# Attention: the low-part score pass on all 128 rows, weighted values 256 columns wide

## The chip, the cores and the metric

The kernel runs on one core of one Trainium2 chip. The metric is the device time of one execution in microseconds, as the median of three runs; the profile is one further execution, whose span runs from its first to its last instruction.

## The reference

Two layers over 256 latent tokens and 256 context tokens of width 1024. Each layer has three branches on one shared projection: an mLSTM, a windowed attention with a sink logit, and a global attention with normalised queries and keys; both attentions have 8 query heads on 2 key heads, head width 64. A gated sum of the branches and a SwiGLU block follow. What the change touches is the middle of both attentions:

```python
scale = d ** -0.5
s = jnp.einsum('bgrqd,bgkd->bgrqk', qblk, k_all).astype(jnp.float32) * scale
p = jax.nn.softmax(s, axis=-1).astype(v_all.dtype)
return jnp.einsum('bgrqk,bgkd->bgrqd', p, v_all)
```

In layer 0 latent queries read all 512 tokens and context queries the 256 context tokens; in layer 1 there are latent queries alone.

## The kernel before

All data is float32. Projections are made of three products of a high and a low part (type F32R, `mm3`): high x high, high x low, low x high. Scores are split in the same way, but a head has 64 features only, so `finish_qk` packs parts by partition. For queries the tile of head group g has the high part on partitions 64 g to 64 g + 63 and the low part on the other half. For keys the tile `k[g]` has the high part of group g on both halves, and one third tile `k2` has the low part of group 0 on partitions 0 to 63 and of group 1 on 64 to 127. `scores` then makes two passes for each group into one PSUM bank: 128 rows (query high and low by key high), and 64 rows (query high by key low).

`attention` walks over units: pair of heads (4), latent or context queries, query block `qb` of 128 queries (2). That is 16 units for each attention in layer 0 and 8 in layer 1, 48 in all. Each unit has two groups g. At each step PE gets the scores of the next unit, the transposes of the last unit's probabilities (`transposed`, into the two PSUM buffers `tr`), some filler (gate projections and merges of other branches, the list `fill`), and the weighted values (`values`). ScalarE copies each transposed tile into a `pt` buffer. `values` multiplies, for each block of 128 keys and each group, a value tile of 64 columns by the transposed probabilities of 128 queries; group 0 goes to PSUM partitions 0 to 63 and group 1 to 64 to 127 of `acc`. These operands are plain float32. After both query blocks `acc` is split into a high and a low part for the merge.

The order on each engine is set once, when the kernel is built: a scheduler takes instructions by priority, and the scores are raised (`urgent`), so they are put between other work, also between the passes of the filler, of the transposes and of the values. On the chip each engine then works through its own list and waits on semaphores. Weight blocks come in by DMA, are split by ScalarE (L192, `whi`) and VectorE (L193, `wlo`), and run ahead of their use. Modulation loads for later use share the pool `q` with queries and keys.

Of the kernel before, what the change touches and what calls it, by code (L numbers as in the profile page):

```python
# [38 lines left out]
# feature blocks of the input projection, in the order in which they are packed  # L39
# [5 lines left out]
# the gates have a bias row only: their weights come apart  # L45
# [3 lines left out]
# columns of the packed shape constants  # L49
# [4 lines left out]
# columns of the packed small parameters  # L54
# [25 lines left out]
class Blank:  # L80
    """Stands for the chip while the order of the weight blocks is collected."""
# [11 lines left out]
class Net:  # L93
    def __init__(self, nc, tc, es, io, out, plan=None):
        self.nc, self.tc, self.io, self.out = nc, tc, io, out
        self.n = 0
        self.plan, self.used, self.sent, self.ready, self.ahead = plan, [], 0, {}, 0
        pool = lambda name, bufs, **kw: es.enter_context(tc.tile_pool(name=name, bufs=bufs, **kw))
        self.cp = pool("cp", 1)
        self.pools = {  # L100
            "wraw": pool("wraw", 5), "wlo": pool("wlo", 8), "whi": pool("whi", 8),
            "hx": pool("hx", 16), "m": pool("m", 9), "y": pool("y", 16), "wk": pool("wk", 5), "pt": pool("pt", 4),
            "q": pool("q", 12), "n": pool("n", 3), "g": pool("g", 2), "h": pool("h", 6),
            "sm": pool("sm", 12), "sn": pool("sn", 6), "sc": pool("sc", 8),
        }
        for name, bufs in (("mm", 3), ("s", 2), ("tr", 2), ("acc", 1)):
            self.pools[name] = pool(name, bufs, space=PSUM)
        self.cst = self.cp.tile([128, NCST], F32, name="cst")
        self.sp = self.cp.tile([128, NSP], F32, name="sp")
        self.X = self.cp.tile([128, NKB, T], F32, name="X")  # L110
        self.hb = self.cp.tile([128, 2, NW_IN - B_O], F32, name="hb")
        self.b1 = self.cp.tile([128, 8], F32, name="b1")
        self.gk = self.cp.tile([128, 52], F32, name="gk")
        self.gqb = self.cp.tile([128, 8], F32, name="gqb")
        self.hmg = self.cp.tile([128, 8], F32, name="hmg")
        self.nsk = self.cp.tile([128, 16], F32, name="nsk")
        self.sel = self.cp.tile([128, 64], F32R, name="sel")
        self.sel2 = self.cp.tile([128, 8], F32R, name="sel2")
        self.dup = self.cp.tile([128, 48], F32, name="dup")
        self.low = self.cp.tile([128, 1], F32, name="low")  # L120
        self.ident = self.cst[:, C_ID:C_ID + 128]
        self.ones = self.cst[:, C_ONE:C_ONE + 1]
        self.bd = self.cst[:, C_BD:C_BD + 2]
        self.cos = self.cst[:, C_COS:C_COS + 256]
        self.sin = self.cst[:, C_SIN:C_SIN + 256]
# [21 lines left out]
    def weights(self, name, idx, kb=8, width=128):  # L147
        """High and low parts of a block in pieces of width columns, fetched in the order in which they are used."""
# [46 lines left out]
    def rms_columns(self, parts, n, inv, cols, nc_):  # L195
        """1 / sqrt(mean + EPS) of every token, up to the factor RS_K that the gains carry, tokens on the partitions.

        parts: squares, features on the partitions; cols: [128, nc_] picks the features of each group."""
# [22 lines left out]
    def inv_rms(self, parts, n, inv, cols, nc_, tag):  # L221
        """The same on all the partitions, tokens along the free axis."""
# [66 lines left out]
    def mod_dve(self, blk):  # L289
        """One block of the modulation: features on the partitions, sums along the free axis."""  # L290
# [109 lines left out]
    def proj_v(self, l, hx):  # L400
        """Values of all the heads of the mLSTM, tokens on the partitions."""
# [15 lines left out]
    def proj_values(self, l, hx):  # L417
        """Values of both attentions, tokens on the partitions: by two blocks of tokens, then by attention."""
# [46 lines left out]
    def finish_qk(self, f, sq, n, gain, keys):  # L465
# [21 lines left out]
        k2 = self.big("q", F32R)  # L487
        c = k2[:, :n]
        for g, x in enumerate((a, b)):
            own = slice(64 * g, 64 * g + 64)  # L490
            for to in (0, 64):
                nc.scalar.activation(out=x[to:to + 64], in_=f[own], func=AF.Copy)
            nc.vector.tensor_tensor(out=c[own], in0=f[own], in1=x[own].bitcast(F32), op=ALU.subtract)
        return hi, lo, k2

# [6 lines left out]
    def gate_part(self, ps, w, k, x):  # L502
        """One feature block of the 16 gate columns; four blocks side by side on the array."""
        r = 32 * (k % 4)
        self.mm(ps[r:r + 32], w[:, 32 * k:32 * k + 32], x, k < 4, k >= 4)
# [54 lines left out]
    def stack_rows(self, rows, n):  # L560
        """Rows as F32R high parts on partitions 0-63 and low parts on 64-127."""
# [10 lines left out]
    def mlstm_weights(self, h, n, rows):  # L572
        """Decay weights by (direction, source block): the tile and the columns that hold them."""
# [53 lines left out]
    def mlstm_heads(self, n, q, k, v, rows, den, other):  # L627
        """Numerators of all the heads; the scores run one half of the source blocks ahead of the values."""
# [33 lines left out]
    def mlstm_sum(self, h, n, nums, r, sums):  # L662
        """Both directions of a head together, and the sums of its squares as rows: high and low parts of a
        row lie 16 partitions apart."""
# [39 lines left out]
    def scores(self, l, pair, q, k, ctx, window, qb):  # L704
        nc = self.nc
# [4 lines left out]
        for g in range(2):  # L710
            ks = slice(64 * g, 64 * g + 64)
# [3 lines left out]
            self.mm(s[:, :nk], q[g][ks, qs], k[2][ks, k0:T], False, True)  # L715
# [25 lines left out]
    def transposed(self, ps, ctx):  # L741
        nk = SEQ if ctx else T
        nb = nk // 128
        pts = []
        for p in ps:
# [3 lines left out]
            pts.append(self.big("pt"))  # L749
            self.nc.scalar.activation(out=pts[-1][:, :nk], in_=pt[:, :nk], func=AF.Copy)  # L750
        return pts

    def values(self, pts, v, window, ctx, qb, acc):
        k0 = SEQ if ctx else 0
        nb = (T - k0) // 128
        for b in range(nb):
            vb = k0 // 128 + b
            c = 256 * (vb % 2) + (0 if window else 128)
            for g in range(2):
                self.mm(acc[64 * g:64 * g + 64, 128 * qb:128 * qb + 128],  # L760
                        v[vb // 2][:, c + 64 * g:c + 64 * g + 64],
                        pts[g][:, 128 * b:128 * b + 128], b == 0, b == nb - 1)

    def attention(self, l, heads, n, ys, fill):
        """heads: (pair, q, k, v, window) by name of the result; one unit of scores runs ahead of the values."""
# [3 lines left out]
        acc = None  # L769
        prev = None  # L770
        done = 0
        for u in range(len(units) + 1):
# [6 lines left out]
            if prev is not None:  # L779
                pts = self.transposed(prev[0], prev[2])  # L780
# [3 lines left out]
            if prev is not None:  # L784
                _, v, ctx, qb, i = prev
                if qb == 0:
                    acc = self.big("acc")
                self.values(pts, *v, ctx, qb, acc)
                if qb == 1:
# [74 lines left out]
    def scaled_hx(self, hx, l, j):  # L864
        """The block before the norm's factor, and the shift as the columns after it."""
# [381 lines left out]
def build(arrays):  # L1247
    nc = bacc.Bacc("TRN2", target_bir_lowering=False, num_devices=1)
# [15 lines left out]
```

## Time and profile before

| | |
|---|---|
| runs | 1526.5, 1526.93, 1527.32 us; median 1526.93 |
| profiled execution | span 1523.1 us, first to last instruction; the median of the runs is 3.8 us more |
| PE (matmul) | busy 1507.0 us, 8999 records |
| VectorE, ScalarE | busy 1067.4 and 748.9 us |
| attention, layer 0 | scores and values from 219 to 492 us |
| attention, layer 1 | from 1106 to 1263 us |

Matmuls overlap in the records: each record lasts from its start to the end of its pipeline, so busy time and mean duration don't say how long PE is kept. The distance between two starts does. In a timeline row "x3" stands for three records of one kind in a row, beginning at the start that is given. A shape "64\*128" in such a row is the rows by columns of the array that are used, and what follows is the output.

### The profile page before, as it was taken

What the parts mean: (1) busy time and instruction counts of PE and PEld (TensorE: products, weight loads), DVE (VectorE), ACT (ScalarE), POOL (GpSimd) and SP (SyncE); (2) the same over time, 40 slices, a digit from 0 to 9 for tenths busy, and PEclk for the clock granted to TensorE, in tenths of its full rate; (3) what the DMA queues carried; (4) which work ended last, traced back from release to release, by engine and by line L of the source; (5) the groups of instructions that cost most, each with busy time, mean ns of one, the idle gap of its engine ahead of it and who ended that gap; (6) DMA issues with size and microseconds to landing.
All of it is one profiled execution on the core that took longest, in us unless ns stands there. A gap on an engine that the chain in (4) does not pass through costs nothing.

```text
span 1523.1 us, 25242 instructions
## 1 busy us (share of the span) xinstructions
PE 1507.0 (99%) x8999; PEld 1241.7 (82%) x9000; DVE 1067.4 (70%) x2664; ACT 748.9 (49%) x1525; POOL 31.1 (2%) x72
## 2 busy tenths in 40 slices
PE   8999999999999999999999999999999999999997
PEld 4586677777777889888888888887788889999997
DVE  5396397666558846889588677654788766776765
ACT  4444455555574334532233233653556665665553
POOL 0001100000000000000000000000100000000000
PEclk9999999999999999999999999999999999999999
DMA  9472012112125632466455553341133335566662
GB/s 333 164 237 76 24 50 91 56 62 63 63 83 180 187 97 78 151 215 209 151 193 185 189 173 118 95 131 57 59 112 111 98 105 160 168 192 182 182 179 91
DMA packets 112591, 203.74 MB, mean 134 GB/s; under 512 B 12496, under 2 KB 16336, under 8 KB 112464
## 3 DMA queue, kind: packets, MB, share of 16 engines
q1 hardware_dynamic: 112464, 202.11, 42.0%
q8 instruction: 71, 1.16, 0.3%
q14 instruction: 56, 0.46, 0.1%
HBM read 201.02 MB, written 1.05 MB: 133 GB/s over the span
## 4 chain that ended last, share of the span: by engine, by line
PE 98%; DVE 1%; ACT 0%; issue 0%; DMA 0%; ACTq 0%; DVEq 0%
PE mm L135 65%; PE s L135 21%; PE acc L135 5%; PE tr L135 4%; PE tr L748 3%; DMA h<-w_if 0%; DVE h L1059 0%; ACT m L372 0%; DVE wlo L193 0%; ACT hx L192 0%; ACT whi L192 0%; DVE y L669 0%; DVE q L485 0%; ACT h L274 0%; PE tr L555 0%
## 5 line engine op out<-in xcount | busy, mean ns | idle before, releaser
L192 ACT ACTIVATE whi<-wraw 128x512 fp32r<-128x512 f32 (+1 forms) x558 | 345.7, 625 | 515.3 <-PE mm L135 352.9
L135 PE MATMUL mm<-hx,whi 128*128 128x512 f32 (+2 forms) x2128 | 548.6, 344 | 1.9 <-ACT hx L192 1.6
L193 DVE TENSOR_TENSOR wlo<-wraw,whi 128x512 fp32r<-128x512 f32 (+1 forms) x558 | 374.4, 681 | 171.8 <-ACT whi L192 159.8
L135 PEld LDWEIGHTS mm<-hx,whi 128*128 128x128 f32 x2128 | 364.6, 189 | 60.8 <-issue 15.0
L135 PE MATMUL mm<-hx,wlo 128*128 128x512 f32 (+2 forms) x1064 | 362.3, 341 | 0.1
L135 PE MATMUL mm<-y,whi 128*128 128x256 f32 (+1 forms) x1024 | 259.7, 332 | 0.0
L135 PEld LDWEIGHTS mm<-hx,wlo 128*128 128x128 f32 x1064 | 201.1, 189 | 26.5 <-issue 4.4
L135 PE MATMUL s<-hx,whi 128*128 128x512 f32 (+2 forms) x800 | 193.5, 331 | 0.0
L135 PEld LDWEIGHTS mm<-y,whi 128*128 128x128 f32 x1024 | 176.6, 190 | 18.5 <-issue 1.5
L135 PE MATMUL mm<-y,wlo 128*128 128x256 f32 (+1 forms) x576 | 188.6, 328 | 0.0
L135 PEld LDWEIGHTS s<-hx,whi 128*128 128x128 f32 x800 | 135.6, 189 | 16.2 <-issue 2.9
L135 PE MATMUL s<-hx,wlo 128*128 128x512 f32 (+2 forms) x400 | 132.6, 332 | 0.5 <-DVE wlo L193 0.5
L135 PEld LDWEIGHTS mm<-y,wlo 128*128 128x128 f32 x576 | 109.5, 190 | 10.0 <-issue 0.5
L298 DVE SCALAR_TENSOR_TENSOR q<-q,q 128x512 f32<-128x512 f32 x160 | 105.4, 689 | 0.1
L298 DVE SCALAR_TENSOR_TENSOR h<-q,q 128x512 bf16<-128x512 f32 x160 | 104.7, 688 | 0.1
L135 PE MATMUL mm<-m,whi 128*128 128x256 f32 (+1 forms) x320 | 85.2, 320 | 0.0
L135 PEld LDWEIGHTS s<-hx,wlo 128*128 128x128 f32 x400 | 75.6, 189 | 10.2 <-issue 2.5
L135 PE MATMUL s<-q,q 128*128 128x512 f32 (+1 forms) x192 | 80.0, 424 | 0.0
L750 ACT ACTIVATE pt<-tr 128x512 f32<-128x512 f32 (+1 forms) x96 | 46.7, 525 | 29.6 <-PE tr L748 29.0
L135 PEld LDWEIGHTS mm<-m,whi 128*128 128x128 f32 x320 | 56.9, 190 | 4.4
L823 DVE SCALAR_TENSOR_TENSOR X<-mm,m,X 128x256 f32<-128x256 f32 x88 | 40.2, 482 | 24.8 <-PE mm L135 24.6
L135 PEld LDWEIGHTS s<-q,q 128*128 128x128 f32 x192 | 36.1, 188 | 24.8 <-issue 21.0
(233 smaller groups left out, 1771.8 us busy)
## 6 DMA issues: line engine op xcount, KB each, us to landing
wraw<-w_ff SPq DMA_DIRECT2D x256, 256.0 KB, 3.0
wraw<-w_in SPq DMA_DIRECT2D x206, 256.0 KB, 2.7
q<-w_mod SPq DMA_DIRECT2D x160, 256.0 KB, 3.0
wraw<-w_br SPq DMA_DIRECT2D x48, 256.0 KB, 2.7
y<-w_mod SPq DMA_DIRECT2D x32, 256.0 KB, 5.4
wraw<-w_o SPq DMA_DIRECT2D x32, 256.0 KB, 2.7
X<-x SPq DMA_DIRECT2D x4, 512.0 KB, 5.3
q<-cc SPq DMA_DIRECT2D x8, 256.0 KB, 4.7
```

The costliest lines, as they stand in the source:

```text
L135: self.nc.tensor.matmul(out, a, b, start=start, stop=stop)
L192: nc.scalar.activation(out=hi, in_=x, func=AF.Copy)
L193: return nc.vector.tensor_tensor(out=lo, in0=x, in1=hi.bitcast(F32), op=ALU.subtract)
L298: nc.vector.scalar_tensor_tensor(out=junk if v == 0 else raw, in0=raw, scalar=1.0, in1=self.cb[v][c], op0=ALU.mult, op1=ALU.mult, accum_ou ...
L748: self.nc.tensor.transpose(pt[:, 128 * b:128 * b + 128], p[:, 128 * b:128 * b + 128], self.ident)
L750: self.nc.scalar.activation(out=pts[-1][:, :nk], in_=pt[:, :nk], func=AF.Copy)
L823: nc.vector.scalar_tensor_tensor(out=self.X[:, j, a:b], in0=ps[:, a - c0:b - c0], scalar=self.mod[l][which][:, j, v:v + 1], in1=self.X[:, ...
```

## The change

`finish_qk` makes two low-part tiles for the keys, one for each group, with the same low part on both halves; `scores` uses all 128 rows in the second pass, so the product of the two low parts is added as well. `attention` keeps the transposed probabilities of both query blocks in one pair of tiles (pool `pv`, two buffers of 1024 columns, blocks of keys by 256 queries), and calls `values` once for both blocks, 256 columns wide. The pool `q` has 15 buffers instead of 12, and a scratch size of the builder is smaller. Comments are dropped.

```diff
-            "q": pool("q", 12), "n": pool("n", 3), "g": pool("g", 2), "h": pool("h", 6),
+            "q": pool("q", 15), "pv": pool("pv", 2), "n": pool("n", 3), "g": pool("g", 2), "h": pool("h", 6),
...
-        k2 = self.big("q", F32R)
-        c = k2[:, :n]
+        lows = [self.big("q", F32R) for _ in range(2)]
         for g, x in enumerate((a, b)):
             own = slice(64 * g, 64 * g + 64)
             for to in (0, 64):
                 nc.scalar.activation(out=x[to:to + 64], in_=f[own], func=AF.Copy)
-            nc.vector.tensor_tensor(out=c[own], in0=f[own], in1=x[own].bitcast(F32), op=ALU.subtract)
-        return hi, lo, k2
+            for to in (0, 64):
+                nc.vector.tensor_tensor(out=lows[g][to:to + 64, :n], in0=f[own], in1=x[own].bitcast(F32),
+                                        op=ALU.subtract)
+        return hi, lo, *lows
...
             self.mm(s[:, :nk], q[g][:, qs], k[g][:, k0:T], True, False)
-            self.mm(s[:, :nk], q[g][ks, qs], k[2][ks, k0:T], False, True)
+            self.mm(s[:, :nk], q[g][:, qs], k[2 + g][:, k0:T], False, True)
...
-    def transposed(self, ps, ctx):
-        nk = SEQ if ctx else T
-        nb = nk // 128
-        pts = []
-        for p in ps:
+    def transposed(self, ps, ctx, qb, pts):
+
+        nb = (SEQ if ctx else T) // 128
+        for p, to in zip(ps, pts):
             pt = self.big("tr")
             for b in range(nb):
                 self.nc.tensor.transpose(pt[:, 128 * b:128 * b + 128], p[:, 128 * b:128 * b + 128], self.ident)
-            pts.append(self.big("pt"))
-            self.nc.scalar.activation(out=pts[-1][:, :nk], in_=pt[:, :nk], func=AF.Copy)
-        return pts
+            self.nc.scalar.activation(
+                out=to.rearrange("p (b q) -> p b q", q=SEQ)[:, :nb, 128 * qb:128 * qb + 128],
+                in_=pt[:, :128 * nb].rearrange("p (b q) -> p b q", q=128), func=AF.Copy)
...
             for g in range(2):
-                self.mm(acc[64 * g:64 * g + 64, 128 * qb:128 * qb + 128],
-                        v[vb // 2][:, c + 64 * g:c + 64 * g + 64],
-                        pts[g][:, 128 * b:128 * b + 128], b == 0, b == nb - 1)
+                self.mm(acc[64 * g:64 * g + 64, :SEQ], v[vb // 2][:, c + 64 * g:c + 64 * g + 64],
+                        pts[g][:, SEQ * b:SEQ * b + SEQ], b == 0, b == nb - 1)
...
             if prev is not None:
-                pts = self.transposed(prev[0], prev[2])
+                if prev[3] == 0:
+                    pts = [self.t("pv", [128, 4 * SEQ]) for _ in range(2)]
+                self.transposed(prev[0], prev[2], prev[3], pts)
...
-                if qb == 0:
+                if qb == 1:
                     acc = self.big("acc")
-                self.values(pts, *v, ctx, qb, acc)
-                if qb == 1:
+                    self.values(pts, *v, ctx, acc)
```

The scores of one unit on PE, in the global attention of layer 0, before. `s` is the score bank, the two `q` behind the arrow are keys and queries, `mm` is a gate projection that serves as filler.

```order
L135 MATMUL s_4225<-q_2257,q_3186 128x512
L135 MATMUL mm_4137<-hx_258,whi_3977 128x512
L135 MATMUL s_4225<-q_2290,q_3186 128x512
L135 MATMUL mm_4137<-hx_259,whi_3977 128x512
L135 MATMUL mm_4137<-hx_258,wlo_3978 128x512
L135 MATMUL mm_4137<-hx_260,whi_3983 128x512
L135 MATMUL mm_4137<-hx_261,whi_3983 128x512
L135 MATMUL mm_4137<-hx_260,wlo_3984 128x512
L135 MATMUL s_4235<-q_2258,q_3187 128x512
L135 MATMUL mm_4137<-hx_262,whi_3983 128x512
L135 MATMUL s_4235<-q_2290,q_3187 128x512
```

The same place after the change:

```order
L135 MATMUL s_4139<-q_2263,q_3152 128x512
L135 MATMUL mm_4055<-hx_257,wlo_3906 128x512
L135 MATMUL s_4139<-q_2296,q_3152 128x512
L135 MATMUL mm_4055<-hx_259,whi_3905 128x512
L135 MATMUL mm_4055<-hx_260,whi_3905 128x512
L135 MATMUL mm_4055<-hx_259,wlo_3906 128x512
L135 MATMUL mm_4055<-hx_261,whi_3905 128x512
L135 MATMUL mm_4055<-hx_262,whi_3905 128x512
L135 MATMUL s_4149<-q_2264,q_3153 128x512
L135 MATMUL mm_4055<-hx_261,wlo_3906 128x512
L135 MATMUL s_4149<-q_2297,q_3153 128x512
```

The order is the same; the second pass of the two groups reads one shared tile before (`q_2290`, half of it each) and two tiles after (`q_2296`, `q_2297`).

The weighted values on PE, a little further on in the same stage, before; `acc` is the output, `pt` the transposed probabilities, `tr` the transposes of the next unit:

```order
L135 MATMUL mm_4137<-hx_266,wlo_3984 128x512
L135 MATMUL acc_4081<-pt_4115,q_2040 64x128
L135 MATMUL acc_4081<-pt_4122,q_2040 64x128
L135 MATMUL acc_4081<-pt_4115,q_2040 64x128
L135 MATMUL acc_4081<-pt_4122,q_2040 64x128
L135 MATMUL acc_4081<-pt_4115,q_2042 64x128
L135 MATMUL acc_4081<-pt_4122,q_2042 64x128
L135 MATMUL acc_4081<-pt_4115,q_2042 64x128
L135 MATMUL acc_4081<-pt_4122,q_2042 64x128
L748 MATMUL tr_4195<-cst,wk_4093 128x128 x2
```

After the change, the values of the same pair of heads and both query blocks:

```order
L135 MATMUL mm_4055<-hx_269,wlo_3912 128x512
L135 MATMUL acc_4081<-pv_3969,q_2046 64x256
L135 MATMUL acc_4081<-pv_3970,q_2046 64x256
L135 MATMUL acc_4081<-pv_3969,q_2046 64x256
L135 MATMUL acc_4081<-pv_3970,q_2046 64x256
L135 MATMUL acc_4081<-pv_3969,q_2048 64x256
L135 MATMUL acc_4081<-pv_3970,q_2048 64x256
L135 MATMUL acc_4081<-pv_3969,q_2048 64x256
L135 MATMUL acc_4081<-pv_3970,q_2048 64x256
L749 MATMUL tr_4116<-cst,wk_4013 128x128 x2
```

Before, such a run stands once for each unit; after, once for two units, with outputs twice as wide, and the next transposes stand behind it in both.

The key preparation on VectorE in layer 0, before and after (`q` is the low part of the keys, `h` another chain):

```order
L193 TENSOR_TENSOR wlo_1928<-wraw_1926,whi_1927 128x512
L493 TENSOR_TENSOR q_1885<-n_1876,q_1878 64x512
L211 TENSOR_SCALAR h_1903<-h_1902 128x256
L193 TENSOR_TENSOR wlo_1982<-wraw_1980,whi_1981 128x512
L493 TENSOR_TENSOR q_1885<-n_1876,q_1879 64x512
L213 TENSOR_TENSOR h_1904<-h_1902,h_1903 128x256
```

```order
L193 TENSOR_TENSOR wlo_1934<-wraw_1932,whi_1933 128x512
L493 TENSOR_TENSOR q_1888<-n_1879,q_1881 64x512 x2
L211 TENSOR_SCALAR h_1909<-h_1908 128x256
L493 TENSOR_TENSOR q_1889<-n_1879,q_1882 64x512 x2
L213 TENSOR_TENSOR h_1910<-h_1908,h_1909 128x256
L193 TENSOR_TENSOR wlo_1988<-wraw_1986,whi_1987 128x512
```

Each copy stands twice, and one weight split has moved behind them.

## Rows read from the trace of the kernel before

**Rows 1.** The page: engine busy time, share and instructions; chain that ended last.

```profile
PE 1507.0 (99%) x8999; PEld 1241.7 (82%) x9000; DVE 1067.4 (70%) x2664; ACT 748.9 (49%) x1525; POOL 31.1 (2%) x72
...
PE 98%; DVE 1%; ACT 0%; issue 0%; DMA 0%; ACTq 0%; DVEq 0%
```

**Rows 2.** Windows: stretch, length, busy us of PE, PEld, DVE, ACT, POOL, clock, DMA share.

```profile
219.00:492.00 273.00, 273.00 (x1502) 202.15 (x1501) 182.26 (x548) 156.58 (x354) 4.16 (x5) 1.00 0.26 83
1100.00:1130.00 30.00, 29.99 (x199) 25.60 (x199) 25.64 (x73) 16.94 (x38) 0.00 (x0) 1.00 0.36 111
```

**Rows 3.** Waits of PE, whole run, longest: total us, times, longest us.

```profile
PE acc L135 <- DVE sn L218: 1.6, 1, 1.6
```

**Rows 4.** Groups of L135 on PE by form: min/median/max ns, first and last start.

```profile
L135 PE MATMUL acc<-pt,q x640: 272/273/324, 250.5 to 1261.9; 128*64 128x128 f32 x160
...
L135 PE MATMUL s<-q,q x192: 276/396/503, 219.6 to 1248.0; 128*128 128x512 f32 x64, 64*128 64x512 f32 x64, 128*128 128x256 f32 x32, 64*128 64x256 f32 x32
```

**Rows 5.** PE's timeline, layer 0, scores among projections: start, length, engine, instruction, count.

```profile
306.46 0.39 PE L135 MATMUL s<-q,q 128*128 128x512 f32 x1
306.69 0.39 PE L135 MATMUL mm<-hx,whi 128*128 128x512 f32 x1
307.00 0.49 PE L135 MATMUL s<-q,q 64*128 64x512 f32 x1
307.43 0.50 PE L135 MATMUL mm<-hx,whi 128*128 128x512 f32 x1
307.77 0.40 PE L135 MATMUL mm<-hx,wlo 128*128 128x512 f32 x1
```

**Rows 6.** PE's timeline, layer 0, scores among transposes.

```profile
251.05 0.33 PE L748 MATMUL tr<-cst,wk 128*128 128x128 f32 x1
251.13 0.36 PE L135 MATMUL s<-q,q 128*128 128x256 f32 x1
251.33 0.27 PE L748 MATMUL tr<-cst,wk 128*128 128x128 f32 x1
251.53 0.38 PE L135 MATMUL s<-q,q 64*128 64x256 f32 x1
251.84 0.88 PE L748 MATMUL tr<-cst,wk 128*128 128x128 f32 x6
```

**Rows 7.** PE's timeline, layer 0, a value run of 8 passes and the projection behind.

```profile
253.08 0.66 PE L135 MATMUL acc<-pt,q 128*64 128x128 f32 x8
253.67 0.73 PE L135 MATMUL mm<-hx,whi 128*128 128x512 f32 x2
254.24 0.39 PE L135 MATMUL mm<-hx,wlo 128*128 128x512 f32 x1
```

**Rows 8.** PE's timeline, layer 0, a value run of 16 passes.

```profile
285.95 0.39 PE L135 MATMUL mm<-hx,wlo 128*128 128x512 f32 x1
286.26 1.09 PE L135 MATMUL acc<-pt,q 128*64 128x128 f32 x16
287.29 0.33 PE L748 MATMUL tr<-cst,wk 128*128 128x128 f32 x1
```

**Rows 9.** PE's timeline, mLSTM of layer 1: float32 passes of 256 columns.

```profile
1065.34 0.59 PE L135 MATMUL acc<-q,y 128*128 128x256 f32 x2
1065.77 1.03 PE L135 MATMUL tr<-wk,y 128*128 128x256 f32 x4
1066.73 0.41 PE L135 MATMUL mm<-q,cst 128*32 128x256 f32 x2
1066.74 0.41 PE L135 MATMUL mm<-wk,cst 128*32 128x256 f32 x2
```

**Rows 10.** Key copies on VectorE, whole run: min/median/max ns.

```profile
L493 DVE TENSOR_TENSOR q<-n,q x8: 674/689/984, 214.8 to 1145.8; 64x512 fp32r<-64x512 f32 x8
```

**Rows 11.** VectorE's timeline, layer 1: a low weight part is written.

```profile
1128.55 0.68 DVE L193 TENSOR_TENSOR wlo<-wraw,whi 128x512 fp32r<-128x512 f32 x1
```

**Rows 12.** PE's timeline, layer 1: the first pass that reads it.

```profile
1132.87 0.38 PE L135 MATMUL mm<-hx,wlo 128*128 128x256 f32 x1
```

## What the change was predicted to do

> **What bounds the kernel now.** I read the page first [rows 1]: TensorE is busy for 1507.0 us, 99% of the span, and 98% of the chain that ended last is PE. The stage windows [rows 2] say the same of the two attention stages that the change touches: from 219 to 492 us (layer 0) PE is busy for 273.00 of 273 us, from 1100 to 1130 us (where that of layer 1 begins; it ends at 1263) for 29.99 of 30, both at a granted clock of 1.00, the 2.4 GHz level. VectorE is busy there for 182.26 of 273 and 25.64 of 30 us. The longest wait of PE in the whole run is one of 1.6 us [rows 3], outside both stages. So PE's own instruction stream sets the end, and what the change is worth is the time by which that stream gets shorter. A busy PE says nothing of that, since matmuls overlap in the records; I therefore read the distance from one start to the next, which I call a slot.
>
> **A 64-row pass in the stream.** The second score pass has 64 rows: 96 of the 192 passes (64 of 512 columns, 32 of 256) [rows 4]. In [rows 5], a plain 512-column pass has a slot of 0.23 us (306.46 to 306.69). The pass ahead of the 64-row one takes 0.31 (306.69 to 307.00), the 64-row one 0.43 (307.00 to 307.43), the one behind it 0.34 (307.43 to 307.77). That is 0.08 + 0.20 + 0.11 = 0.39 us above three plain slots. The new second pass has 128 rows and the same columns, so its nearest row is the first pass of the same scores at 306.46, with its plain slot, and I take the 0.39 as wholly saved there.
>
> Not every one of the 96 stands among projections. In the built order of before 62 have a projection behind them, 22 a transpose and 12 a pass of weighted values. Between transposes [rows 6] a 128-row and a 64-row pass stand in the same position: the transpose ahead has a slot of 0.08 (251.05 to 251.13) and 0.20 (251.33 to 251.53), the pass itself 0.20 (251.13 to 251.33) and 0.31 (251.53 to 251.84), 0.23 us more in all. The first of the two follows a value run, which may lengthen it, so 0.23 is the lower bound and 0.39 the upper; I take the middle, 0.31. Ahead of values I count the pass's own 0.20 alone, because the values pay for an entry of their own either way. The sum: 62 x 0.39 = 24.2, 22 x 0.31 = 6.8, 12 x 0.20 = 2.4, together **33.4 us**. Bounds: 96 x 0.39 = 37.4 above; below, 24.2 + 22 x 0.23 + 12 x 0.10 = 30.5.
>
> **Weighted values.** Today 320 instructions of 128 columns, two array passes each, as the 640 records in [rows 4] say. The two heads stand on different column halves of the array. A run of 8 passes takes 0.59 us to the next start [rows 7] (253.08 to 253.67), one of 16 takes 1.03 [rows 8] (286.26 to 287.29): 0.44 us for 8 passes more, 0.055 each, half of what one 128-column pass of this type takes by itself (0.215 for 256 columns [rows 9]). So the passes of two heads run side by side, 0.11 us a pair, and 0.15 is fixed. The slot ahead of a run is 0.31 instead of 0.23 (285.95 to 286.26, +0.08), and with a projection behind, its first two slots take 0.57 [rows 7] (253.67 to 254.24) instead of 2 x 0.23, +0.11. A run thus costs 0.34 above its streaming, or 0.23 where a transpose follows (transposes have an entry anyway).
>
> The built order has 63 such runs before and 30 after. Before: 19 x 0.34 + 44 x 0.23 = 16.6; after: 12 with a projection behind and 18 with a transpose, 4.1 + 4.1 = 8.2. Saved: 8.4, of which I take 7.7, since 6 of the 19 end in a 64-row pass whose entry is counted above. Streaming: 160 pairs of instructions, 2 x 0.11 each, 35.2 us before; after 80 pairs of 256 columns. No row shows a 64-column value pass of 256 columns; its nearest row is a 128-column pass in the same f32 type, 0.43 us for two, 0.215 each (1065.34 to 1065.77) [rows 9], so 80 x 2 x 0.215 = 34.4. That two stand side by side at this width too is what the last lines of [rows 9] show for 32-column passes of 256 columns: those of one tile start at 1066.73, those of the other at 1066.74, two each. A run that a score pass cuts at an odd count leaves one head's two passes without a partner, so they take the time of two pairs, 0.22 us, for half the work. The order has 24 odd runs before (24 x 0.11 = 2.6 us lost) and 8 after at double width (8 x 0.215 = 1.7). Streaming saves 0.8 + 0.9 = 1.7. Values together: **9.4 us**, between 6.9 (33 runs at 0.23 less the shared entries, nothing in streaming) and 12.9 (33 runs at 0.34 and 1.7).
>
> **What is added.** The key preparation gains 8 VectorE copies (two for each of four calls; the 8 that exist take 0.689 us each [rows 10]), 5.5 us in all. ScalarE's 96 copies out of PSUM now write blocks of columns that stand apart; no row has that form, so I bound it between nothing and 0.5 us more each, 48 us over both stages, on an engine that has 273 - 156.58 = 116 us free in layer 0 alone [rows 2]. Both lie beside PE work and cost nothing while leads hold. The tightest lead I found is in layer 1: VectorE ends a low weight part at 1128.55 + 0.68 = 1129.23 [rows 11], and PE first reads it at 1132.87 [rows 12], 3.6 us later. By then PE has shed the five 64-row passes that the order puts ahead of it, 2.0 us, and VectorE has taken on two copies, 1.4 us: 3.4 of 3.6 are gone, and with the 1.4 us of the second key call some 10 us on it can turn into a wait. I add **1 us**, from 0 to 3 (two such places at 1.4).
>
> The attention probabilities now sit in one pair of tiles for two query blocks, so ScalarE's copies of the next pair wait until the values have been read. In the built order the value run stands ahead of those transposes on PE, so I cost that at 0; the price where it isn't so is the last rival. The larger pool moves some modulation loads up the DMA queue, ahead of weight loads; the queue's transfers keep DMA at 0.26 busy in layer 0 [rows 2], and I cost it at 0.
>
> **Sum.** 33.4 + 9.4 - 1 = 41.8 us off the profiled span of 1523.1, giving 1481.3. The median of the runs lies 3.8 us above that span (1526.93), so 1526.9 - 41.8 = **1485 us**. With all bounds on one side: 37.4 + 12.9 - 0 = 50, 1477; and 30.5 + 6.9 - 3 = 34.4, 1492.5.
>
> **A rule against the size.** The rows give 0.39 us for a 64-row pass. The Trainium skill, TensorEngine Tiling (Array Packing), Key Properties, says that changing the tiling mode drains TensorE, which agrees in sign. Its page TensorE: Matmul & The Clock Gate, Part 2, puts the pipe drain at about 128 cycles; at 2.4 GHz an estimate by that is 0.053 us for each change, so 96 x 2 x 0.053 + 33 x 2 x 0.053 = 13.7 us, which would give 1513. In [rows 5] the three slots lose 0.39 us for two changes, nearly four times the estimate, and the measurement decides.
>
> **Rivals.**
> *Only the edges go.* The 0.20 in the 64-row pass's own slot might belong to adding the low parts into a bank just written, and not to its shape; then it stays with the 128-row pass. Price: 96 x 0.20 = 19.2 us of the gain, 1504 us. Against it: projection passes, which also add one after the other into one bank, have plain slots [rows 5]. It is here too that the drain estimate of the page would end, with its 1513. Chance 0.07.
> *Wide values run one behind the other.* If 64-column passes of 256 columns did not overlap, 320 passes at 0.215 would take 68.8 instead of 34.4 us, and the total would be 1485 + 34 = 1519, still 0.5% faster. [rows 9] speaks against it. Chance 0.03.
> *VectorE becomes the bound in layer 1.* From 1100 to 1130 us it is busy for 25.64 of 30 us [rows 2]. The order puts 16 of the 64-row passes into the first 90 us of that stage: 16 x 0.35 (33.4 / 96) and some runs, 7 us of PE time less, and 1.4 to 2.8 us more on VectorE. At that load 77 + 2 of 83 us, 95%, would be busy. If its in-order queue can't be filled so densely, what PE saved there comes back, 1485 + 7 = 1492, and up to 1496 if the same holds for a few us more. Chance 0.10.
> *Slower: the single pair of probability tiles.* If PE met the next pair's transposes ahead of the value run, it would hold both transpose buffers and wait for the run and a copy, 8 x 0.215 + 0.15 and some 0.6 for the copy, 2.5 us, 24 times (16 pairs of units in layer 0, 8 in layer 1): 60 us, so 1485 + 60 = 1545. It outweighs the gain from 1.8 us a pair on. The order speaks against it. Chance 0.02.
>
> **Chances.** Forecast 0.78, the rivals 0.07, 0.03, 0.10 and 0.02. The forecast's own bounds are 1477 to 1492; taking in the VectorE case makes it 1477 to 1496, which leaves out 0.12 and the tails. About 0.2% (3 us) is what a measurement of this kernel can tell from no change. All cases but the last end over 0.2% faster; I leave 0.02 for a loss of nearly all of the gain: faster 0.96, same 0.02, slower 0.02.
>
> **What would show it.** Right: plain slots of 0.23 us around the 512-column score passes among projections; 320 value records of 256 columns in 30 runs, a run of 16 taking near 16 / 2 x 0.215 + 0.15 = 1.87 us; attention stages shorter by some 28 us in layer 0 and 14 in layer 1, all else equal in length; still no waits of PE. Wrong: slots behind the second score pass still at 0.43 (first rival), value passes that start 0.2 us apart (second), PE waits on VectorE from 1100 us on (third), waits of ScalarE's PSUM copies on PE with PE idle behind them (fourth).

## The result, and the profile of the changed kernel

The changed kernel takes 1483.79 us (median of four runs, 1482.15 to 1484.2); before takes 1527.12 beside it. The ratio is 0.9715, 95% interval 0.9703 to 0.9727: 2.8% faster, 43.3 us. The prediction was 1485, range 1477 to 1496. The profiled execution has a span of 1480.4 us, where before has 1523.1.

The page of the changed kernel: engine busy time, share and instructions, and the chain that ended last (compare [rows 1]).

```profile
span 1480.4 us, 24591 instructions
...
PE 1464.5 (99%) x8680; PEld 1226.4 (83%) x8680; DVE 1066.2 (72%) x2672; ACT 744.5 (50%) x1525; POOL 30.9 (2%) x72
...
PE 94%; DVE 3%; ACT 1%; issue 1%; DMA 1%; SPq 0%; ACTq 0%; DVEq 0%
```

PE has 42.5 us less to do and is still busy for 99% of the span: its stream sets the end as before, and is shorter. Its share of the chain went from 98 to 94%, that of VectorE from 1 to 3%. PE's records are fewer by the value passes, 320 in place of 640 (one record of before is missing in its trace).

Windows of the changed kernel, columns as in [rows 2]: the attention stage of layer 0, and two stretches of that of layer 1.

```profile
219.00:472.00 253.00, 253.00 (x1354) 200.10 (x1353) 199.06 (x611) 157.55 (x360) 3.92 (x5) 1.00 0.34 111
1087.00:1117.00 30.00, 30.00 (x233) 27.41 (x233) 27.81 (x87) 22.00 (x48) 1.60 (x2) 1.00 0.42 133
1117.00:1147.00 30.00, 29.93 (x237) 28.01 (x237) 28.56 (x95) 22.72 (x56) 1.60 (x2) 1.00 0.46 149
```

PE has next to no gap (0.07 us in the last stretch), at the same granted clock of 1.00. VectorE has come closer to its limit: 28.56 of 30 us in layer 1, where [rows 2] show 25.64 at the stage's start.

Waits of PE in the changed kernel, whole run, longest first (us in total, times, longest us); compare [rows 3].

```profile
PE acc L135 <- DVE sn L218: 1.6, 1, 1.6
PE mm L135 <- ACT hx L192: 1.6, 1, 1.6
PE mm L135 <- DVE dup L1121: 1.5, 1, 1.5
```

None of these is in the two stages. The change made no new wait of PE.

Groups of PE in the changed kernel by form, columns as in [rows 4]: value passes and score passes.

```profile
L135 PE MATMUL acc<-pv,q x320: 378/379/431, 255.4 to 1218.4; 128*64 128x256 f32 x160
...
L135 PE MATMUL s<-q,q x192: 277/393/501, 219.8 to 1204.3; 128*128 128x512 f32 x128, 128*128 128x256 f32 x64
```

All 192 score passes now have 128 rows; the 320 value records have 256 columns (two records for each instruction). PE's timeline of the changed kernel shows what that does to the slots, first two score passes that stand behind projections (as in [rows 5], at an earlier place of the stage), then a run of 16 value passes (as in [rows 8]), then a value run that two scores cut up.

```profile
225.28 0.40 PE L135 MATMUL mm<-hx,whi 128*128 128x512 f32 x1
225.51 0.40 PE L135 MATMUL s<-q,q 128*128 128x512 f32 x1
225.75 0.39 PE L135 MATMUL mm<-hx,whi 128*128 128x512 f32 x1
225.98 0.40 PE L135 MATMUL s<-q,q 128*128 128x512 f32 x1
226.21 0.40 PE L135 MATMUL tr<-h,sel 128*128 128x256 f32 x2
...
322.44 1.95 PE L135 MATMUL acc<-pv,q 128*64 128x256 f32 x16
324.32 0.66 PE L749 MATMUL tr<-cst,wk 128*128 128x128 f32 x4
...
287.65 0.39 PE L135 MATMUL mm<-hx,wlo 128*128 128x512 f32 x1
287.97 0.65 PE L135 MATMUL acc<-pv,q 128*64 128x256 f32 x2
288.55 0.49 PE L135 MATMUL s<-q,q 128*128 128x512 f32 x1
288.97 0.65 PE L135 MATMUL acc<-pv,q 128*64 128x256 f32 x2
289.55 0.49 PE L135 MATMUL s<-q,q 128*128 128x512 f32 x1
```

Each of these two scores has a slot of 0.23 to 0.24 us (225.51 to 225.75, 225.98 to 226.21), and so have the projections ahead of them and between them: the 0.31, 0.43 and 0.34 of [rows 5] are gone. The run of 16 takes 1.88 (322.44 to 324.32). The last rows show what is left of the price: value passes use 64 columns of the array, so a score between them still has a slot of 0.42 (288.55 to 288.97).

**Where the time came from.** From the start of the first score to the start of the last value pass, layer 0 takes 271.0 us before and 241.1 after, layer 1 takes 155.8 and 142.1; what lies between the stages takes 615.5 and 615.3. That is 29.9 + 13.7 = 43.6 us. Adding up PE's slots in both stages by what starts them gives nearly the same, 42.7 us, in another cut: score passes 61.9 before, 43.5 after; projections 271.7 and 259.8; transposes 35.5 and 29.3; value passes 47.1 and 40.9. The scores' own slots give 18.4 us. Projections and transposes, whose own work the change leaves as it is, give 18.1: a pass just ahead of or behind one of another shape carries part of the price, as [rows 5] show.

### The profile page after: what moved, and what is told of

Its sections match the earlier page's. It is cut to its first block, busy times and chain, and to the rows that moved or that the text cites. A ratio compares the mean times of both kernels' runs of the same rounds, so it can differ in the third digit from the quotient of the medians.

```text
span 1480.4 us, 24591 instructions
## 1 busy us (share of the span) xinstructions
PE 1464.5 (99%) x8680; PEld 1226.4 (83%) x8680; DVE 1066.2 (72%) x2672; ACT 744.5 (50%) x1525; POOL 30.9 (2%) x72
## 4 chain that ended last, share of the span: by engine, by line
PE 94%; DVE 3%; ACT 1%; issue 1%; DMA 1%; SPq 0%; ACTq 0%; DVEq 0%
PE mm L135 63%; PE s L135 20%; PE tr L135 5%; PE acc L135 4%; PE tr L749 2%; DVE wlo L193 1%; DMA X<-x 0%; DVE wk L730 0%; DVE h L1060 0%; DMA h<-w_if 0%; ACT hx L192 0%; DVE h L444 0%; ACT h L372 0%; DVE q L485 0%; DVE wk L739 0%
## 5 line engine op out<-in xcount | busy, mean ns | idle before, releaser
L135 PE MATMUL mm<-hx,whi 128*128 128x512 f32 (+2 forms) x2128 | 541.9, 342 | 1.9 <-ACT hx L192 1.6
L135 PEld LDWEIGHTS mm<-hx,whi 128*128 128x128 f32 x2128 | 365.0, 189 | 54.1 <-issue 8.6
L135 PE MATMUL mm<-hx,wlo 128*128 128x512 f32 (+2 forms) x1064 | 361.1, 340 | 0.0
L135 PE MATMUL mm<-y,whi 128*128 128x256 f32 (+1 forms) x1024 | 260.4, 332 | 0.0
L135 PEld LDWEIGHTS mm<-hx,wlo 128*128 128x128 f32 x1064 | 201.1, 189 | 26.1 <-issue 4.3
L135 PE MATMUL s<-hx,whi 128*128 128x512 f32 (+2 forms) x800 | 193.5, 331 | 0.0
L135 PEld LDWEIGHTS mm<-y,whi 128*128 128x128 f32 x1024 | 176.8, 190 | 17.2
L135 PE MATMUL mm<-y,wlo 128*128 128x256 f32 (+1 forms) x576 | 188.6, 327 | 0.0
L135 PEld LDWEIGHTS s<-hx,whi 128*128 128x128 f32 x800 | 135.6, 189 | 16.3 <-issue 2.9
L135 PE MATMUL s<-hx,wlo 128*128 128x512 f32 (+2 forms) x400 | 132.6, 332 | 0.5 <-DVE wlo L193 0.5
L135 PEld LDWEIGHTS mm<-y,wlo 128*128 128x128 f32 x576 | 109.4, 190 | 9.6
L135 PE MATMUL mm<-m,whi 128*128 128x256 f32 (+1 forms) x320 | 85.2, 320 | 0.0
L135 PEld LDWEIGHTS s<-hx,wlo 128*128 128x128 f32 x400 | 75.6, 189 | 10.2 <-issue 2.5
L135 PE MATMUL s<-q,q 128*128 128x512 f32 (+1 forms) x192 | 66.1, 385 | 0.1
L135 PEld LDWEIGHTS mm<-m,whi 128*128 128x128 f32 x320 | 56.9, 190 | 4.4
L749 PE MATMUL tr<-cst,wk 128*128 128x128 f32 x320 | 49.4, 276 | 0.1
L135 PE MATMUL mm<-whi,hx 128*128 128x256 f32 (+1 forms) x192 | 49.5, 319 | 0.0
```

The lines of the kernel that those rows point to most:

```text
L135: self.nc.tensor.matmul(out, a, b, start=start, stop=stop)
L749: self.nc.tensor.transpose(pt[:, 128 * b:128 * b + 128], p[:, 128 * b:128 * b + 128], self.ident)
```

## The experiments

Ratios are to the kernel before, run on the same chip, with 95% intervals. "Stages" are those of the paragraph above.

### One part at a time

The first kernel is before with the new scores alone.

```diff
-        k2 = self.big("q", F32R)
+        lows = [self.big("q", F32R) for _ in range(2)]
...
+            for to in (0, 64):
+                nc.vector.tensor_tensor(out=lows[g][to:to + 64, :n], ...)
...
-            self.mm(s[:, :nk], q[g][ks, qs], k[2][ks, k0:T], False, True)
+            self.mm(s[:, :nk], q[g][:, qs], k[2 + g][:, k0:T], False, True)
```

> The kernel before with the score part of the change alone: low key parts on both halves, second pass on 128 rows, pool q at 15; values as before. Theory (a 64-row pass costs 0.39 us above plain slots where projections stand around it, 33.4 us for the 96): 1527.1 - 33.4 = 1494 us, no 0.43 us slot left at a score pass, no new wait of PE. Rival 'only the edges go' (the 0.20 us in the pass's own slot belongs to the second addition into the bank): 1527.1 - 14 = 1513 us and the second pass keeps a slot of 0.43 us.

Measured: 1494.12 us, ratio 0.9787 (0.9772 to 0.9802), stages 250.7 and 143.9. The prediction's term for the scores was 33.4 us; 1527.0 - 1494.1 = 32.9.

The second is the changed kernel with the old keys and the old 64-row pass, which leaves the wide values alone.

```diff
-            self.mm(s[:, :nk], q[g][:, qs], k[2 + g][:, k0:T], False, True)
+            self.mm(s[:, :nk], q[g][ks, qs], k[2][ks, k0:T], False, True)
```

> The kernel before with the value part alone: probabilities of two query blocks in one pair of tiles, values 256 columns wide; second score pass on 64 rows, one shared tile of low key parts, pool q at 12. Theory (what is saved is the number of value runs, 63 to 31 in this order, and odd runs, 24 to 10): 1527.1 - 9 = 1518 us. Rival (the parts overlap: the value run saves little as long as 64-row score passes cut into it): 1524 us or more.

Measured: 1518.01 us, ratio 0.9943 (0.9927 to 0.996), stages 264.0 and 153.4. The term was 9.4; 1527.0 - 1518.0 = 9.0.

The third keeps the new keys too, with their copies on VectorE, and goes back in the pass alone.

```diff
-            self.mm(s[:, :nk], q[g][:, qs], k[2 + g][:, k0:T], False, True)
+            self.mm(s[:, :nk], q[g][ks, qs], k[2 + g][ks, k0:T], False, True)
```

> The changed kernel with the second score pass back on 64 rows, all else as changed: the 8 added VectorE copies and the larger pool stay, so it has their cost without the gain for which they are there. Theory (copies hidden): 1518 us, like the value part alone within 2 us; against the changed kernel 33 us more. Rival (the copies and the moved loads cost on the path): 3 to 5 us above the value part alone.

Measured: 1517.09 us, ratio 0.9938 (0.9923 to 0.9953), stages 263.2 and 153.2. It agrees with the second within the intervals, and lies 33.3 us above the changed kernel, from which it differs in the pass alone. So the gain of the scores is in the number of rows that the pass uses; the other layout of the keys and the larger pool give nothing, and the eight copies cost nothing there. The two parts alone sum to 32.9 + 9.0 = 41.9 us, and together they gave 43.3: they add up within the intervals.

### Is the price one of each pass, or of the change of shape?

This kernel keeps the 64-row passes and puts those of the two head groups next to each other, so that the array changes its shape half as often. It is before with this edit in `scores`:

```diff
+        ss = [self.big("s") for _ in range(2)]
         for g in range(2):
-            ks = slice(64 * g, 64 * g + 64)
+            first = nc.tensor.matmul(ss[g][:, :nk], q[g][:, qs], k[g][:, k0:T], start=True, stop=False)
+        with self.urgent(URGENT), self.after(first):
+            for g in range(2):
+                ks = slice(64 * g, 64 * g + 64)
+                self.mm(ss[g][:, :nk], q[g][ks, qs], k[2][ks, k0:T], False, True)
+        for g in range(2):
             head = 4 * g + pair
-            s = self.big("s")
-            self.mm(s[:, :nk], q[g][:, qs], k[g][:, k0:T], True, False)
-            self.mm(s[:, :nk], q[g][ks, qs], k[2][ks, k0:T], False, True)
+            s = ss[g]
```

> The kernel before, with 64-row passes kept but the two of a unit made neighbours on PE: both 128-row passes first, then both 64-row passes (47 of 48 units stand so in the order). Value runs go from 63 to 55, odd runs from 24 to 8, transpose blocks from 83 to 65 by the way, worth about 6 us. Theory (the price hangs on the change of shape, one in and one out, not on the pass): 47 x 0.36 + 6 = 23 us less, 1504 us, and further down to 1495 us if the two passes, on different row halves, also run side by side. Rival 'only the edges go' (0.20 us belongs to each second pass): 47 x 0.19 + 6 = 15 us less, 1512 us. Against all: the first group's scores now wait for the second group's bank; PE waits would show that.

Measured: 1499.74 us, ratio 0.9815 (0.9801 to 0.9828), stages 251.5 and 146.5. PE's timeline of this kernel, layer 0 (columns as in [rows 5]):

```profile
304.99 0.40 PE L135 MATMUL mm<-hx,whi 128*128 128x512 f32 x1
305.22 0.40 PE L712 MATMUL s<-q,q 128*128 128x512 f32 x1
305.55 0.49 PE L135 MATMUL s<-q,q 64*128 64x512 f32 x2
305.97 0.50 PE L135 MATMUL mm<-hx,wlo 128*128 128x512 f32 x1
306.31 0.64 PE L135 MATMUL mm<-hx,whi 128*128 128x512 f32 x2
```

Two 64-row passes ("x2") take 0.42 us to the next start (305.55 to 305.97), where one alone takes 0.43 in [rows 5]. In the unmerged records the 47 pairs of the kernel start 0.003 to 0.004 us apart: one uses rows 0 to 63, the other rows 64 to 127, and they run at the same time. The slots ahead (0.33) and behind (0.34) are near those of a single pass (0.31 and 0.34). So the price is paid once for each visit to the other shape. The result is near what follows from that: 47 visits fewer, at 33.4 / 96 = 0.35 us from the prediction's sum, are 16.4 us, and 47 passes that lie beside another are 31 x 0.23 + 16 x 0.12 = 9.1 us; together 25.5, and some 6 more for the runs and blocks that the new order joins, 31.5. Measured: 1528.8 - 1499.7 = 29.0 (this chip's run of before is 1528.76). It fell between the two values that had been written down for it. By PE's slots in the stages, scores and projections lost 23.0 us and transposes and values 5.6, so it is the first part that came out short, by 2.5. No new wait of PE came up. The 128-row pass still saves more, 32.9 us against 29.0, each against before on its own chip, without any help from the order; the two intervals just meet.

### How much room is left on VectorE?

The prediction's third rival was that VectorE becomes the bound in layer 1. In the changed kernel PE does not wait, but the rows show how near that is. VectorE's timeline of the changed kernel, where a low weight part is written:

```profile
1086.30 0.68 DVE L193 TENSOR_TENSOR wlo<-wraw,whi 128x512 fp32r<-128x512 f32 x1
```

PE's timeline of the changed kernel, where it is first read:

```profile
1087.18 0.40 PE L135 MATMUL mm<-hx,wlo 128*128 128x512 f32 x1
```

It is ready at 1086.98 and read at 1087.18: a lead of 0.2 us, where the least near there was 3.8 before. In the first 40 us of the stage in layer 0 the least lead went from 2.5 to 0.9. To see what happens when it is used up, this kernel makes every low-part copy of the keys twice: 16 VectorE copies more, 11 us, in the whole run, where the change itself had added 8.

```diff
-            for to in (0, 64):
+            for to in (0, 64, 0, 64):
```

> The changed kernel with every low-part copy of the keys made twice: 16 copies of 0.69 us more on VectorE, 11 us in all, twice what the change added. Theory (VectorE's work lies beside PE's): same as the changed kernel, 1483.8 within 1.5 us. Rival (VectorE is near its limit early in layer 1): 2.8 us for each of four key calls less what slack is left, 3 to 8 us more, with waits of PE on VectorE near 1090 to 1130 us.

Measured: 1492.71 us, ratio 0.9768 (0.9755 to 0.9781), 8 to 9 us slower than the changed kernel. I had expected no change; the rival was right, with a size a little above its 3 to 8 us. The stages take 243.6 and 146.7 us, 2.5 and 4.6 more. Windows of this kernel in layer 1:

```profile
1087.00:1117.00 30.00, 29.00 (x202) 25.23 (x201) 27.77 (x85) 20.06 (x45) 1.61 (x2) 1.00 0.31 100
1117.00:1147.00 30.00, 29.01 (x228) 26.02 (x226) 27.95 (x89) 20.64 (x50) 1.36 (x2) 1.00 0.43 133
```

Its longest waits of PE:

```profile
PE s L135 <- ACT wk L732: 2.2, 5, 0.6
PE acc L135 <- DVE sn L218: 1.6, 1, 1.6
```

PE now has gaps of 1 us in each 30, and the first wait is new: a score pass waits for its PSUM bank, which is free only when the softmax of an earlier unit has read it (`wk`, ScalarE at L732, which waits for VectorE). The least lead of a low weight part is 0.06 us in both layers: PE reads it as soon as it is written. The waits that the view names are 2.2 us for the score bank. PE's gaps in both stages sum to 4.2 us, where the changed kernel has 0.2, and the stages lost 7.1; the rest lies in slots that got longer and is not assigned to a cause.

The extra copies do two things: they load VectorE, and they make the keys ready later. The next kernel does a part of the second without the first: ScalarE rewrites each low part in place after VectorE's copies.

```diff
+            for to in (0, 64):
+                nc.scalar.activation(out=lows[g][to:to + 64, :n],
+                                     in_=lows[g][to:to + 64, :n].bitcast(F32), func=AF.Copy)
```

> The changed kernel with 16 copies of the low key parts onto themselves added on ScalarE, behind the VectorE copies: the keys are ready some 1.3 us later in each call, as in the kernel with doubled VectorE copies (1492.7 us, 7 us of the stages lost), but VectorE has no more work. Theory (VectorE's load took those 7 us): same as the changed kernel within 2 us. Rival (the keys' lateness took them, whatever engine copies): 5 to 8 us slower than the changed kernel.

Measured: 1485.02 us, ratio 0.9726 (0.9712 to 0.974), stages 241.1 and 142.1, as in the changed kernel. The changed kernel run again beside it:

> The changed kernel itself again, as the mark for the two beside it on the same chip. Every theory: 0.9715 of the kernel before, about 1484 us.

Measured: 1483.58 us, ratio 0.9713 (0.97 to 0.9726). So sixteen more copies cost 7 to 9 us on VectorE and nothing that can be told on ScalarE.

The expectation took the two kernels to make the keys equally late, and they don't. Measured from a pass of PE that lies ahead of them, the last low part of each of the four key calls is ready 2.5 to 4.0 us later than in the changed kernel where VectorE copies, and 0.7 to 1.5 us later where ScalarE does. So a lateness of up to 1.5 us costs nothing; a longer one wasn't tried by itself. What speaks against it is that no wait of PE on a key copy is named in either kernel, while the new wait is one for the softmax, in which VectorE has a part. That VectorE's time was scarce, and not the moment at which the keys are ready, is the likely cause, and not a shown one.

If VectorE's time is what was scarce, moving the change's own added copies away from VectorE might free something. In this kernel VectorE writes each low part once and ScalarE makes the second copy.

```diff
-            for to in (0, 64):
-                nc.vector.tensor_tensor(out=lows[g][to:to + 64, :n], in0=f[own], in1=x[own].bitcast(F32),
-                                        op=ALU.subtract)
+            nc.vector.tensor_tensor(out=lows[g][own, :n], in0=f[own], in1=x[own].bitcast(F32), op=ALU.subtract)
+            other = slice(64 - 64 * g, 128 - 64 * g)
+            nc.scalar.activation(out=lows[g][other, :n], in_=lows[g][own, :n].bitcast(F32), func=AF.Copy)
```

> The changed kernel with the second half of each low key part copied by ScalarE from the first, so VectorE has the 8 copies of before and ScalarE 8 more. The order of PE's runs is the same (30 value runs, 87 transpose blocks). Theory (in the changed kernel VectorE's lead over PE at both key calls is nearly used up, 0.2 and 0.9 us at the least, but not overdrawn): same as the changed kernel, at best 1 us faster, with a least lead of 1.5 us or more. Rival (the added VectorE copies do cost on the path there): 3 us faster or more.

Measured: 1484.09 us, ratio 0.9716 (0.9703 to 0.9729), no different. Its windows:

```profile
1087.00:1117.00 30.00, 29.96 (x218) 27.16 (x218) 26.02 (x81) 21.56 (x48) 1.42 (x2) 1.00 0.36 114
1117.00:1147.00 30.00, 30.00 (x243) 27.54 (x243) 29.21 (x98) 23.50 (x58) 1.52 (x2) 1.00 0.43 138
```

VectorE has more room in the first stretch (26.02 against 27.81), the least lead there goes from 0.2 to 2.7 us, and PE, which did not wait before, gains nothing. In the second stretch VectorE is no less busy (29.21 against 28.56). Room on an engine off the path is worth something only when the next change takes it.

### Can fewer changes of shape be had from the order?

A score pass that lies within a value run cuts it, and pays (0.42 us in the rows above). How early the scores stand is set by one number, the priority that `urgent` gives. Three kernels are the changed one with another value of it.

```diff
-URGENT = 50
+URGENT = 200
```

> The changed kernel with the priority of scores raised from 50 to 200, which changes the order alone: blocks of transposes on PE 87 to 52, value runs 30 to 27, odd runs 8 to 4. Theory (PE's stream sets the end and every change of kind in it costs a fixed time; about 0.10 us for a block of transposes, 0.34 for a value run, 0.215 for an odd run): 35 x 0.10 + 3 x 0.34 + 4 x 0.215 = 5.4 us less, 1478 us. Rival (scores that are put earlier wait for a score bank and hold PE): 1484 us or more, with waits of PE on VectorE or ScalarE.

Measured: 1496.96 us, ratio 0.9807 (0.9793 to 0.9822): 13 us slower, where I expected 5 us faster. Its windows in both layers:

```profile
228.00:479.00 251.00, 248.74 (x1305) 191.48 (x1304) 190.94 (x585) 154.59 (x347) 4.51 (x5) 1.00 0.35 110
1090.00:1242.00 152.00, 149.97 (x1132) 132.72 (x1131) 120.50 (x345) 102.32 (x225) 3.91 (x5) 1.00 0.37 115
```

Its longest waits of PE:

```profile
PE s L135 <- ACT wk L732: 1.8, 5, 0.5
PE acc L135 <- DVE sn L218: 1.6, 1, 1.6
```

PE has gaps in both stages, 4.3 us together, and the longest wait is again that of a score pass for its bank: the order puts the scores ahead of the point at which a bank is free. The slots of projections just ahead of a group's first score pass are 0.26 us on average (90 of them), 0.19 in the changed kernel (60): some 6 us, part of the gaps among them. That doesn't make up the loss. From the end of the input phase on, PE's slots by what starts them are 10.1 us longer for projections and 3.0 for transposes, although the transposes stand in fewer blocks; scores and values give back 2.7. With 100 in place of 200:

> The changed kernel with the priority of scores at 100, order alone: transpose blocks 87 to 64, value runs 30 to 28, odd runs 8 to 6. Theory by the fixed prices: 23 x 0.10 + 2 x 0.34 + 2 x 0.215 = 3.4 us less, 1480 us. Rival (as at 200, scores stand ahead of a free bank and PE waits): between 1484 and the 1497 us of priority 200.

Measured: 1492.08 us, ratio 0.9762 (0.9749 to 0.9775). The longest waits:

```profile
PE s L135 <- ACT wk L732: 2.7, 5, 0.9
PE acc L135 <- DVE sn L218: 1.6, 1, 1.6
```

The same wait is named, and its sum is larger than at 200 (2.7 us against 1.8) where the loss is smaller, so the named waits don't measure the loss. And with 20:

> The changed kernel with the priority of scores at 20 instead of 50, order alone: transpose blocks 87 to 66, value runs 30 to 29, odd runs 8 to 10. Theory (a fixed price for each change of kind, scores not early enough to wait): 21 x 0.10 + 0.34 - 2 x 0.215 = 2 us less, 1482 us. Rival (the softmax comes later and PE waits for it): 1485 us or more.

Measured: 1487.26 us, ratio 0.9733 (0.972 to 0.9747). The interval meets that of the changed kernel (0.9703 to 0.9727), so it is the same or a little slower, and not faster as I expected. Its stages, 238.1 and 140.5, are 4.6 us shorter together than those of the changed kernel, but in part only because the first scores stand later in the order: what lies between the stages takes 618.7 us, 3.4 more. From one and the same instruction behind the input phase to the end, it takes 1303.0 us against 1301.3. Why the later scores don't gain anything isn't settled.

My theory for these three was a fixed price for each change of kind in the order, so that another order would save 2 to 5 us. It fell: at 100 and 200 scores wait for a bank, which is a part of the loss and not shown to be all of it, and at 20 no gain came out. No kernel here beats the changed one.

## Why the prediction was right

**The bound.** It rested on PE's stream setting the end, so that the gain is what that stream sheds. PE's busy share stayed at 99%, its busy time fell by 42.5 us and the span by 42.7.

**The 64-row pass.** The term was 33.4 us; alone it gave 32.9. The 0.39 us of [rows 5], in three slots, is gone from all three, although the 128-row pass adds into a bank just written as the 64-row one did. That settles the first rival (*only the edges go*, 1504): the price of the middle slot belonged to the shape too. The paired 64-row passes say more closely that it is paid once for each visit. Pricing a visit from one place in [rows 5], a second in [rows 6] and a middle between them was a rough way; that it came out within 0.5 us owes something to chance.

**The drain estimate.** Three slots lose 0.39 us for one visit, and the gain of the scores alone is 32.9 us. The Trainium skill, TensorEngine Tiling (Array Packing), Key Properties, says that a change of the tiling mode drains TensorE; the runs agree in sign. The 13.7 us that the prediction estimated from the pipe drain in the Trainium skill, TensorE: Matmul & The Clock Gate, Part 2, is a third of the 43.3 measured.

**Weighted values.** The term was 9.4; alone it gave 9.0. The run of 16 takes 1.88 us, predicted 1.87, and there are 30 runs: the passes of two heads do lie side by side at 256 columns (in that run each pair starts within 0.007 us), which settles the second rival (1519). How the 9.0 us divide between fewer runs (7.7) and fewer odd ones (1.7) wasn't tried apart.

**What was added.** The prediction put 1 us on waits. It was 0: no wait of PE in either stage. The rows from which it came are not a pair. By the program's buffers, the pass of [rows 12] reads a part that VectorE had ended at 1121.25, and the part of [rows 11], ended at 1129.23, is first read at 1154.51. The tightest lead of layer 1 is 3.8 us, from 1118.17 to 1121.93, so the 3.6 of the prediction was near it by luck; the 2.5 of layer 0, which is tighter, was overlooked. PE's timeline of before:

```profile
1121.93 0.39 PE L135 MATMUL mm<-hx,wlo 128*128 128x512 f32 x1
...
1154.51 0.28 PE L135 MATMUL mm<-y,wlo 128*128 128x256 f32 x1
```

The idea that leads get used up was right in its direction, since the least leads shrank to 0.9 and 0.2 us. The third rival (*VectorE becomes the bound in layer 1*, 1492) is near what the kernel with 16 copies more ran into, 1492.7, and in layer 0 too; that the numbers agree is chance, since the rival priced PE time that comes back and not added copies. Where between 0 and 11 us of added VectorE work the loss begins wasn't tried.

**The single pair of probability tiles.** PE does not wait for the copies of the next pair, as the order had it; the rival of 1545 did not come up. That more buffers would make no difference wasn't tried, and rests on the absent waits.

**The stages.** Predicted 28 us in layer 0 and 14 in layer 1, all else equal; measured 29.9 and 13.7, and 0.2 between. The total of 41.8 was 1.5 short of 43.3: plus 1.0 for the wait that did not come, plus 1.4 that the two parts gave together beyond their sum, minus 0.9 by which the parts alone fell short of their terms. All of these are within the interval of the measurement (0.0012, or 1.8 us, to either side), so that the sum came so close is in part luck.

## What to carry to other kernels

Read a matmul's cost from the distance between starts, with the slots ahead of and behind it: a pass that uses half of the array pays in its neighbours' slots as well as in its own, and filling the other half, even with a product that matters little, can be the cheaper way. Group what must use part of the array, and pair it with a partner on the other half. When the engine that bounds gets faster, look at the least lead of each feeder, buffer by buffer, and not at its mean load alone: here it went to 0.2 us unseen, and the next 11 us of feeder work cost 7 to 9.

## What the runs showed of the hardware

- Two 64-row passes on different halves of the rows, one right behind the other and into different PSUM banks, start 0.003 to 0.004 us apart and take 0.42 us together, as long as one alone (0.43). I had known this only of passes on different columns [rows 9].
- A visit to the 64-row shape costs 0.08 to 0.10 us in the slot ahead, some 0.20 in its own and 0.11 in the slot behind (512 columns, among projections), for two passes side by side as for one.
- A score pass of 128 rows between value passes of 64 columns has a slot of 0.42 us, among projections 0.23: its own slot loses 0.19 to the change of columns, about as much as a 64-row pass loses in its own.
- The first 100 us differ between executions. The first score pass starts at 219.8 us in one profile of the changed kernel and at 221.7 in the other, and at 224.9 in that of the paired passes. The windows of these three (columns as in [rows 2]) show a granted clock of 1.00, 0.98 and 0.91 there, and 1.00 from 100 to 230 us in all three. DMA moves less there too (the last column, in GB/s), and which of the two comes first isn't shown. So stage times tell an effect of 2 us better than the total does.

The changed kernel, first profile:

```profile
0.00:100.00 100.00, 94.99 (x473) 58.03 (x474) 59.20 (x142) 49.11 (x85) 0.20 (x4) 1.00 0.70 247
```

The changed kernel, second profile:

```profile
0.00:100.00 100.00, 95.23 (x464) 57.43 (x466) 57.72 (x137) 48.86 (x85) 0.20 (x4) 0.98 0.69 242
```

The paired 64-row passes:

```profile
0.00:100.00 100.00, 96.26 (x451) 56.65 (x452) 54.09 (x130) 46.23 (x81) 0.20 (x4) 0.91 0.67 232
```
